# The head of a decoder layer: weight splits placed between evictions of normalised rows, a tile of x fetched sooner, normalisation moved to ScalarE

## The chip, the core and the metric

The kernel runs on one core of one Trainium2 chip. The time is that of one execution on the device, in microseconds, as the median of several runs. A core has a matrix engine (TensorE, PE in the profile), VectorE (DVE), ScalarE (ACT), GpSimd (POOL), a queue for transfers (SyncE, SP) and 16 DMA engines. Each engine works through its own list of instructions in order; semaphores connect the lists.

## The reference

One layer of a hybrid decoder in float32, 512 tokens of width 1024. The input is normalised, and the normalised rows `h` go through one wide input projection, whose columns are split among gated linear attention, latent attention and gates; an MLP and two more normalisations follow.

```python
def layer_norm(x, g, b):
    mu = jnp.mean(xf, axis=-1, keepdims=True)
    var = jnp.mean(jnp.square(xf - mu), axis=-1, keepdims=True)
    return ((xf - mu) * lax.rsqrt(var + LN_EPS) * g + b).astype(x.dtype)
...
h = layer_norm(x, ln_in_g, ln_in_b)
...
q_g, k_g, v_g, r_g, a_lr, q_lat, kv_lat, gate_logits = jnp.split(h @ w_in, offsets, axis=-1)
```

The change touches only what happens up to the first of these projections: the normalisation of the input, its transposition, and the preparation of the first weights.

## The kernel before

**Tiles.** The 512 tokens are four tiles of 128 rows and 1024 columns, `xt[0]` to `xt[3]`. TensorE needs the normalised rows transposed, so that the 1024 channels stand in eight blocks `k` of 128 partitions. `hT[k]` holds block `k` for all 512 tokens, as two matrices: `h` is kept as a high part, rounded to the matrix engine's float format (fp32r), and a low part, the rest. Weights are kept the same way. Each product is three matmuls: high by high, high by low and low by high (in the first projection lines 284, 285 and 286).

**Normalising a tile** (`ln_rows`, L428). VectorE takes the statistics of both halves of the row (L431), joins them (L432) and adds epsilon (L433); GpSimd takes the power -1/2 (L434). Then the row is scaled: on VectorE in one instruction (L440), or, with `on_act`, on ScalarE (L438) after VectorE has made the bias (L437). Before the change tile 0 goes to ScalarE and the others to VectorE.

**Transposing** (`ln_transpose`, L442). For two tiles at a time (256 tokens) and for each block `k`, two transposes (L449) fill a PSUM bank, named `px`, or `mm` for `k` = 4 and 5 of the first two tiles. Four `px` banks and four `mm` banks exist. Then the bank is evicted: ScalarE writes the high part of `hT[k]` with gain and bias (L452, tile `h`), a second copy `lnt` in full precision comes from VectorE (L456) or, in the first two tiles at odd `k`, from ScalarE (L454), and VectorE subtracts the two for the low part (L457).

**Weights.** `stream` is the list of all weight pieces in the order of use. `fetch(n)` asks for the transfers of the first `n` on the SP queue (L176, tile `wraw`, three buffers); `pump(i)` makes the splits as far as allowed ahead of piece `i`: ScalarE rounds the high part (L191), VectorE subtracts for the low part (L192). The first projection (`lat`, 720 columns in two parts of 360, in four pieces of two blocks each) keeps its eight split pieces in `xh` and `xl`; later pieces go to `whi` and `wlo`. A `wraw` buffer is free for the next transfer when both splitting instructions have read it. `st["gates"]` lists instructions behind which the next split has to stand on its engine; `tc.issue_after` does this.

**The order.** The code is traced once. A planner that comes with the language gives every engine its list from this order and from its own estimates of time, so an instruction that is written later can stand earlier on its engine if nothing binds it. Generators such as `ln_in1` are advanced one step between groups of matmuls (`tick`). The code of the head is, in this order: `pump(-1)` (L470: two pieces fetched and split), `ln_in0` (L471: tiles 0 and 1 normalised, transposed and evicted), three copies of the unit matrix (L474 to L477), then the first projection for tiles 0 and 1, under which `ln_in1` (L1098) loads tiles 2 and 3, normalises and transposes them, and then the same projection for tiles 2 and 3. `prep` (L496) makes masks and the tables of the rotary embedding; its first instructions are bound behind `last_in`, the low part of block 3 of tiles 0 and 1.

Of the kernel before, what the change touches and what calls it, by code (L numbers as in the profile page):

```python
# [19 lines left out]
P = 128  # L20
# [32 lines left out]
def tile_hybrid_block(ctx: ExitStack, tc: tile.TileContext, I, out, dbg=None):  # L53
# [39 lines left out]
    def f(ap):  # L93
        return ap.bitcast(F32)
# [39 lines left out]
    identr = consts.tile([P, P], F32R, name="identr")  # L134
# [5 lines left out]
    st = {"dma": 0, "spl": 0, "gates": ()}  # L140
# [38 lines left out]
    def pump(i):  # L179
        fetch(i + 1 + DMA_AHEAD)  # L180
        while st["spl"] < min(len(stream), i + 2 + SPLIT_AHEAD):
            e = stream[st["spl"]]
            if st["spl"] > i + e.get("ahead", SPLIT_AHEAD) and not e["res"]:
                break
            nk, n = e["nk"], e["n"]
            hi, lo = [A([P, nk, T * 2 // nk], F32R, w) for w in HOME["a" if e["res"] else e.get("home", "w")]]
            raw = e["src"]() if "src" in e else e.pop("raw")
            with ExitStack() as gates:
                for g in st["gates"]:
                    gates.enter_context(tc.issue_after(g.ins))  # L190
                st["ins"] = act(hi[:, :nk, :n], raw[:, :nk, :n], AF.Copy)  # L191
                st["lo"] = vtt(lo[:, :nk, :n], raw[:, :nk, :n], f(hi[:, :nk, :n]), op=ALU.subtract)  # L192
            st["gates"] = ()
            e["w"] = (hi, lo)
            if "post" in e:
                e["post"](raw)
            if "post2" in e:
                later[st["spl"] + 2] = lambda p=e["post2"], r=raw: p(r)
            later.pop(st["spl"], lambda: None)()
            st["spl"] += 1  # L200
# [227 lines left out]
    def ln_rows(src, dst, mv, on_act=False):  # L428
# [4 lines left out]
        vts(mv[:, 1:2], mv[:, 1:2], LN_EPS, None, op0=ALU.add)  # L433
        gtt(mv[:, 1:2], mv[:, 1:2], mhalf[:, 0:1], op=ALU.pow)  # L434
        if on_act:
            nmr = S([P, 1], F32, "nmr")
            stt(nmr, mv[:, 0:1], -1.0, mv[:, 1:2], op0=ALU.mult, op1=ALU.mult)  # L437
            act(dst, src, AF.Identity, scale=mv[:, 1:2], bias=nmr)  # L438
        else:
            vts(dst, src, mv[:, 0:1], mv[:, 1:2], op0=ALU.subtract, op1=ALU.mult)  # L440

    def ln_transpose(rows, g, b, outs, hf, alt=False, n="h0"):  # L442
        tk = slice(hf * 256, (hf + 1) * 256)
        for k in range(NK):
# [7 lines left out]
            ha = act(hi, p[:, :256], AF.Identity, scale=g[:, k:k + 1], bias=b[:, k:k + 1])  # L452
            if (alt or n == "h1") and k % 2:
                act(tmp, p[:, :256], AF.Identity, scale=g[:, k:k + 1], bias=b[:, k:k + 1])  # L454
            else:
                vts(tmp, p[:, :256], g[:, k:k + 1], b[:, k:k + 1], op0=ALU.mult, op1=ALU.add)  # L456
            hd = vtt(lo, tmp, f(hi), op=ALU.subtract)  # L457
            if n == "h1":
                st["ln"] = (ha, hd)
            yield hd  # L460
# [4 lines left out]
    def ln_in0():  # L465
        for tt in range(2):
            ln_rows(xt[tt], xt[tt], mvin[:, tt, :], on_act=tt == 0)
        yield from ln_transpose(xt, g_in, b_in, hT, 0, alt=True)

    pump(-1)  # L470
    last_in = list(ln_in0())[3]  # L471


    act(identr, ident, AF.Copy)  # L474
# [21 lines left out]
    def prep():  # L496
        with tc.issue_after(last_in.ins):
# [600 lines left out]
    def ln_in1():  # L1098
        for i in range(4):
            if i == 0:  # L1100
                load_x(2)
            if i == 2:
                load_x(3)
            yield
        with tc.issue_after(last_in.ins):
            for tt in (2, 3):
                ln_rows(xt[tt], xt[tt], mvin[:, tt, :])
        yield
        yield from ln_transpose(xt, g_in, b_in, hT, 1, alt=False)
# [604 lines left out]
```

## Time and profile before

| | us |
|---|---|
| median of 3 runs | 872.87 |
| lowest and highest of them | 872.13, 873.47 |
| the profiled execution, its own time | 873.01 |
| span of the profiled execution, first to last instruction | 871.2 |
| PE busy | 854.2 |
| VectorE busy | 635.0 |
| ScalarE busy | 470.6 |

The profile is of one execution. Its span is 1.8 us shorter than the time of the same execution. Times in its views count from the start of the span. In a timeline row stand the start, the time that the merged instructions took, the engine, the line and operation, and out<-in by the names of the tiles; in square brackets the idle time of the engine before it and what ended it. In a group's row stand, behind the bar, the busy time, the mean of one in ns, and the idle time ahead of the group. In a row of the waits stand the total, the number and the longest.

### The profile page before, as it was taken

To read this page: it belongs to the slowest core of one execution; us is meant where nothing else is said; L and a number is where in the kernel's file an instruction comes from. 1 tells how busy PE (TensorE), PEld (TensorE's weight loads), DVE (VectorE), ACT (ScalarE), POOL (GpSimd) and SP (SyncE) were. 2 spreads that over 40 slices of the span, in tenths; PEclk is the share of its full clock that TensorE was granted. 3 is DMA by queue.
4 is the path that set the end of the run, shared out by engine and by line. 5 is a ranking of instruction groups with operands and counts; after the bars stand their busy time and mean duration, and the time that the engine had idled before them with its cause. 6 is when DMAs were issued, how large, how long until landed. Compare 5 with 4: busy or idle time off the path is not lost.

```text
span 871.2 us, 12821 instructions
## 1 busy us (share of the span) xinstructions
PE 854.2 (98%) x4757; PEld 746.3 (86%) x4757; DVE 635.0 (73%) x1045; ACT 470.6 (54%) x829; POOL 146.0 (17%) x184
## 2 busy tenths in 40 slices
PE   5999999999999999999999999999999999999996
PEld 5988888889999988888888888988888888889985
DVE  7859989978567547567766887986567646888865
ACT  6546777656475625355545333575366446666820
POOL 0323304221110030300000022005300520141000
PEclk9999999999999999999999999999999999999999
DMA  7994946695656434322126445008922990499311
GB/s 243 280 238 146 324 161 169 169 320 189 145 156 155 148 93 121 79 62 97 49 96 252 140 144 216 1 0 240 264 77 49 284 223 24 98 242 229 114 67 73
DMA packets 95214, 134.58 MB, mean 154 GB/s; under 512 B 12672, under 2 KB 58112, under 8 KB 95152
## 3 DMA queue, kind: packets, MB, share of 16 engines
q1 hardware_dynamic: 73840, 92.36, 33.2%
q0 software_dynamic: 19392, 37.76, 20.4%
q10 hardware_dynamic: 1920, 3.66, 1.1%
q8 instruction: 37, 0.61, 0.3%
q14 instruction: 25, 0.20, 0.1%
HBM read 110.15 MB, written 8.91 MB: 137 GB/s over the span
## 4 chain that ended last, share of the span: by engine, by line
PE 97%; DVE 1%; ACT 1%; DMA 1%; POOLq 0%; issue 0%; SPq 0%; DVEq 0%
PE mm L248 11%; PE mm L249 11%; PE mm L250 11%; PE mm L286 5%; PE mm L285 5%; PE mm L284 5%; PE mm L1240 4%; PE mm L1239 4%; PE mm L1238 4%; PE px L1527 2%; PE px L1525 2%; PE px L1526 2%; PE mm L1527 2%; PE mm L1525 2%; PE mm L1526 2%; PE mm L755 1%
## 5 line engine op out<-in xcount | busy, mean ns | idle before, releaser
L192 DVE TENSOR_TENSOR wlo<-wraw,whi 128x1024 fp32r<-128x1024 f32 (+1 forms) x90 | 98.7, 1098 | 83.2 <-ACT whi L191 75.0
L191 ACT ACTIVATE whi<-wraw 128x1024 fp32r<-128x1024 f32 (+1 forms) x90 | 85.5, 950 | 80.9 <-PE mm L249 42.7
L249 PE MATMUL mm<-h,whi 128*128 128x512 f32 x224 | 87.2, 389 | 0.0
L248 PE MATMUL mm<-h,whi 128*128 128x512 f32 x224 | 86.9, 390 | 0.0
L250 PE MATMUL mm<-h,wlo 128*128 128x512 f32 x224 | 83.4, 390 | 0.0
L192 DVE TENSOR_TENSOR wlo<-wq,whi 128x1024 fp32r<-128x1024 f32 x44 | 53.8, 1223 | 28.4 <-ACT whi L191 28.1
L1544 POOL DMA_DIRECT2D res<-ev x42 | 37.4, 1018 | 181.8 <-ACT ev L1542 148.3
L191 ACT ACTIVATE whi<-wq 128x1024 fp32r<-128x1024 f32 x44 | 46.5, 1058 | 27.4 <-PE mm L1239 17.1
L1240 PE MATMUL mm<-sh,wlo 128*128 128x256 f32 x176 | 50.0, 284 | 0.0
L1238 PE MATMUL mm<-sh,whi 128*128 128x256 f32 x176 | 50.0, 284 | 0.0
L1239 PE MATMUL mm<-sh,whi 128*128 128x256 f32 x176 | 49.8, 283 | 0.0
L250 PEld LDWEIGHTS mm<-h,wlo 128*128 128x128 f32 x224 | 42.0, 188 | 9.1 <-DVE wlo L192 0.4
L249 PEld LDWEIGHTS mm<-h,whi 128*128 128x128 f32 x224 | 42.1, 188 | 8.8
L248 PEld LDWEIGHTS mm<-h,whi 128*128 128x128 f32 x224 | 42.1, 188 | 8.6
L191 ACT ACTIVATE xh<-wraw 128x1024 fp32r<-128x1024 f32 (+1 forms) x28 | 27.1, 981 | 28.5 <-PE mm L286 16.5
L192 DVE TENSOR_TENSOR xl<-wraw,xh 128x1024 fp32r<-128x1024 f32 (+1 forms) x28 | 31.2, 1128 | 7.7 <-ACT xh L191 7.7
L1587 ACT ACTIVATE relu<-mm 128x512 f32<-128x512 f32 x24 | 14.2, 594 | 41.2 <-PE mm L250 41.2
L1240 PEld LDWEIGHTS mm<-sh,wlo 128*128 128x128 f32 x176 | 33.8, 192 | 0.0
L1239 PEld LDWEIGHTS mm<-sh,whi 128*128 128x128 f32 x176 | 33.8, 192 | 0.0
L1238 PEld LDWEIGHTS mm<-sh,whi 128*128 128x128 f32 x176 | 33.8, 192 | 0.0
L1238 PE MATMUL mm<-h,whi 128*128 128x256 f32 x112 | 32.0, 286 | 0.0
L1240 PE MATMUL mm<-h,wlo 128*128 128x256 f32 x112 | 31.9, 284 | 0.0
(495 smaller groups left out, 2701.2 us busy)
## 6 DMA issues: line engine op xcount, KB each, us to landing
wraw<-in_w_ff_dram SPq DMA_DIRECT2D x36, 512.0 KB, 4.8
wraw<-in_w_in_dram SPq DMA_DIRECT2D x30, 512.0 KB, 4.7
wq<-in_w_ff_dram POOLq DMA_DIRECT2D x26, 512.0 KB, 9.8
res<-ev POOLq DMA_DIRECT2D x42, 256.0 KB, 9.2
wq<-in_w_in_dram SPq DMA_DIRECT2D x20, 512.0 KB, 7.3
wq<-in_w_in_dram POOLq DMA_DIRECT2D x18, 512.0 KB, 9.8
hsd<-hs SPq DMA_DIRECT2D x16, 256.0 KB, 4.1
xr<-hsd SPq DMA_DIRECT2D x16, 256.0 KB, 5.1
```

The source lines that it names most:

```text
L191: st["ins"] = act(hi[:, :nk, :n], raw[:, :nk, :n], AF.Copy)
L192: st["lo"] = vtt(lo[:, :nk, :n], raw[:, :nk, :n], f(hi[:, :nk, :n]), op=ALU.subtract)
L248: mm(o, hi[:, c], xh, start=k == 0, stop=False)
L249: mm(o, hi[:, c], xl, start=False, stop=False)
L250: mm(o, lo[:, c], xh, start=False, stop=k == nk - 1)
L284: mm(o, xh, hi[:, :n], start=opens, stop=False, skip_group_check=share)
L285: mm(o, xh, lo[:, :n], start=False, stop=False, skip_group_check=share)
L286: mm(o, xl, hi[:, :n], start=False, stop=last, skip_group_check=share)
L1238: mm(oa, hi[:, k, c], xh, start=opens and k == 0 and a == 0, stop=False, skip_group_check=True)
L1239: mm(oa, hi[:, k, c], xl, start=False, stop=False, skip_group_check=True)
L1240: mm(oa, lo[:, k, c], xh, start=False, stop=k == 3, skip_group_check=True)
L1544: nc.gpsimd.dma_start(res[tt + t][:, j * T:(j + 1) * T], e, accum_op=ALU.add)
```

## The change

- `split_next` is cut out of `pump`: it makes one split. Ahead of the first normalisation there is one split instead of two, while three pieces are fetched instead of two.
- Tile 2 of x is asked for right behind these three (`load_x(2)`), ahead of the fourth weight piece, and tile 3 at the first step of `ln_in1`.
- `st["turns"]` is a list of gates, one for each coming split: split 1 stands behind the eviction of block 1 of tiles 0 and 1 (on both engines), split 2 behind that of block 3, split 3 behind that of block 5, split 4 is free. Later ones are bound behind the statistics of tiles 2 and 3 and behind blocks 3 and 5 of these tiles' evictions.
- In the first two tiles the evictions are bound to their written order on each engine (`run` in `ln_transpose`).
- `ln_rows` has `to`: columns below it are scaled on VectorE, the others on ScalarE. Tile 0 goes to ScalarE whole, tile 1 is cut in half, tiles 2 and 3 go to ScalarE whole.
- `lnt` of odd blocks comes from ScalarE for tiles 2 and 3 too.
- The statistics of tiles 2 and 3 are bound behind the low half of the split that was traced last; `prep` is bound behind the low part of the last block of tiles 2 and 3.
- `identr`, a copy of the unit matrix that nothing reads, is gone.

```diff
-    st = {"dma": 0, "spl": 0, "gates": ()}
+    st = {"dma": 0, "spl": 0, "gates": (), "turns": []}
...
+            split_next()
+
+    def split_next():
+        e = stream[st["spl"]]
+        nk, n = e["nk"], e["n"]
+        if st["turns"]:
+            st["gates"] = st["turns"].pop(0)
...
-    def ln_rows(src, dst, mv, on_act=False):
+    def ln_rows(src, dst, mv, to=D):
...
-        vts(mv[:, 1:2], mv[:, 1:2], LN_EPS, None, op0=ALU.add)
+        var = vts(mv[:, 1:2], mv[:, 1:2], LN_EPS, None, op0=ALU.add)
         gtt(mv[:, 1:2], mv[:, 1:2], mhalf[:, 0:1], op=ALU.pow)
-        if on_act:
+        if to < D:
             nmr = S([P, 1], F32, "nmr")
             stt(nmr, mv[:, 0:1], -1.0, mv[:, 1:2], op0=ALU.mult, op1=ALU.mult)
-            act(dst, src, AF.Identity, scale=mv[:, 1:2], bias=nmr)
-        else:
-            vts(dst, src, mv[:, 0:1], mv[:, 1:2], op0=ALU.subtract, op1=ALU.mult)
+            act(dst[:, to:], src[:, to:], AF.Identity, scale=mv[:, 1:2], bias=nmr)
+        if to:
+            vts(dst[:, :to], src[:, :to], mv[:, 0:1], mv[:, 1:2], op0=ALU.subtract, op1=ALU.mult)
+        return var
 
     def ln_transpose(rows, g, b, outs, hf, alt=False, n="h0"):
         tk = slice(hf * 256, (hf + 1) * 256)
+        done = {}
+
+        def run(fn, *a, **kw):
+            with ExitStack() as gates:
+                if alt and fn in done:
+                    gates.enter_context(tc.issue_after(done[fn].ins))
+                i = fn(*a, **kw)
+            done.update({act: i} if fn is act else {vts: i, vtt: i})
+            return i
...
-            ha = act(hi, p[:, :256], AF.Identity, scale=g[:, k:k + 1], bias=b[:, k:k + 1])
-            if (alt or n == "h1") and k % 2:
-                act(tmp, p[:, :256], AF.Identity, scale=g[:, k:k + 1], bias=b[:, k:k + 1])
+            ha = run(act, hi, p[:, :256], AF.Identity, scale=g[:, k:k + 1], bias=b[:, k:k + 1])
+            if k % 2:
+                ha = run(act, tmp, p[:, :256], AF.Identity, scale=g[:, k:k + 1], bias=b[:, k:k + 1])
             else:
-                vts(tmp, p[:, :256], g[:, k:k + 1], b[:, k:k + 1], op0=ALU.mult, op1=ALU.add)
-            hd = vtt(lo, tmp, f(hi), op=ALU.subtract)
+                run(vts, tmp, p[:, :256], g[:, k:k + 1], b[:, k:k + 1], op0=ALU.mult, op1=ALU.add)
+            hd = run(vtt, lo, tmp, f(hi), op=ALU.subtract)
...
-            ln_rows(xt[tt], xt[tt], mvin[:, tt, :], on_act=tt == 0)
+            ln_rows(xt[tt], xt[tt], mvin[:, tt, :], to=tt * T)
         yield from ln_transpose(xt, g_in, b_in, hT, 0, alt=True)
 
-    pump(-1)
-    last_in = list(ln_in0())[3]
-
-
-    act(identr, ident, AF.Copy)
+    fetch(3)
+    load_x(2)
+    split_next()
+    evs = list(ln_in0())
+    last_in = evs[7][1]
+    st["turns"] = [evs[k] for k in (1, 3, 5)] + [()]
...
     def prep():
+        last_in = evs[-1][1]
...
     def ln_in1():
-        for i in range(4):
-            if i == 0:
-                load_x(2)
-            if i == 2:
-                load_x(3)
-            yield
-        with tc.issue_after(last_in.ins):
-            for tt in (2, 3):
-                ln_rows(xt[tt], xt[tt], mvin[:, tt, :])
-        yield
-        yield from ln_transpose(xt, g_in, b_in, hT, 1, alt=False)
+        load_x(3)
+        yield
+        for tt, wait in ((2, 3), (3, 2)):
+            for _ in range(wait):
+                yield
+            with tc.issue_after(st["lo"].ins):
+                st["turns"].append((ln_rows(xt[tt], xt[tt], mvin[:, tt, :], to=0),))
+        st["turns"].append(())
+        yield
+        for k, e in enumerate(ln_transpose(xt, g_in, b_in, hT, 1, alt=False)):
+            evs.append(e)
+            if k in (3, 5):
+                st["turns"].append(e)
+            yield
```

34 lines of the change are left out of this document (16 added, 18 removed).

## The prediction

> **What bounds the kernel now.** I read the page first. Its first part says that TensorE is busy in nearly all of the span:
>
> ```profile
> PE 854.2 (98%) x4757; PEld 746.3 (86%) x4757; DVE 635.0 (73%) x1045; ACT 470.6 (54%) x829; POOL 146.0 (17%) x184
> ```
>
> 871.2 us of span less 854.2 leaves 17 us. A busy PE need not be at its peak, so the view of the waits comes next, for PE alone and over the whole span:
>
> ```profile
> PE px L449 <- ACT x L438: 8.8, 1, 8.8
> PE px L1046 <- DVE PT L112: 0.4, 1, 0.4
> PE mm L248 <- ACT h L452: 0.3, 1, 0.3
> PE mm L248 <- DVE rt L1000: 0.2, 1, 0.2
> PE px L449 <- DVE lnt L456: 0.2, 1, 0.2
> ```
>
> PE waits 8.8 us for the first normalised tile, 0.2 us more in the head (for the evictions `lnt`), and 0.9 us in all the rest of the program. Whatever the change moves, it can win only where PE isn't already fed, and that is before about 15 us. So the head is read in order of time, PE's timeline first (start, time with the modelled end, engine, line, what):
>
> ```profile
> 8.81 1.11 PE L449 MATMUL px<-ca,x 128*128 128x128 f32 x4 [8.81 <-ACT x L438]
> 9.71 0.63 PE L449 MATMUL mm<-ca,x 128*128 128x128 f32 x2
> 10.22 1.11 PE L449 MATMUL px<-ca,x 128*128 128x128 f32 x4
> ...
> 11.41 0.65 PE L284 MATMUL mm<-xh,h 128*128 128x360 f32 x1
> 11.86 0.50 PE L285 MATMUL mm<-xl,h 128*128 128x360 f32 x1
> 12.16 0.50 PE L284 MATMUL mm<-xh,h 128*128 128x360 f32 x1
> 12.46 0.50 PE L285 MATMUL mm<-xl,h 128*128 128x360 f32 x1
> 13.13 1.14 PE L449 MATMUL px<-ca,x 128*128 128x128 f32 x4 [0.17 <-DVE lnt L456]
> 13.92 0.82 PE L286 MATMUL mm<-xh,h 128*128 128x360 f32 x2
> 14.57 0.33 PE L284 MATMUL mm<-xh,h 128*128 128x360 f32 x1
> 14.74 0.33 PE L285 MATMUL mm<-xl,h 128*128 128x360 f32 x1
> ```
>
> Two things are to be seen. First, the pace: from start to start a 360-column matmul takes 0.30 us at 11.86 and 12.16, and 0.17 us at 14.57. Up to about 14.3 us PE goes at half pace, whatever it is given. Second, the gaps at that pace: 11.41 to 11.86 is 0.45 (0.15 too long), 12.46 to 13.13 is 0.67 (0.37 too long), and from 13.13 to 14.57, where four transposes and two matmuls stand, some 0.15 are lost. Before 10.22 about 0.1 is lost: two transposes at 0.23 each, (9.71 - 8.81) / 4, from 9.71 would be over at 10.16, and the matrix waits for tile 1. In all 0.75 us of waiting, at half pace.
>
> What they wait for stands in the timelines of ScalarE and VectorE:
>
> ```profile
> 7.51 1.24 ACT L438 ACTIVATE x<-x,nmr,mvin 128x1024 f32<-128x1024 f32 x1 [2.14 <-DVE nmr L437]
> 8.66 2.17 ACT L191 ACTIVATE xh<-wraw 128x720 fp32r<-128x720 f32 x3
> 10.74 1.92 ACT L452 ACTIVATE h<-px,ca 128x256 fp32r<-128x256 f32 x4
> ...
> 13.44 1.05 ACT L454 ACTIVATE lnt<-px,ca 128x256 f32<-128x256 f32 x2
> ```
>
> ```profile
> 9.18 0.98 DVE L440 TENSOR_SCALAR x<-x,mvin 128x1024 f32<-128x1024 f32 x1 [0.67 <-POOL mvin L434]
> 10.09 2.53 DVE L192 TENSOR_TENSOR xl<-wraw,xh 128x720 fp32r<-128x720 f32 x3
> 12.54 0.99 DVE L456 TENSOR_SCALAR lnt<-px,ca 128x256 f32<-128x256 f32 x2
> 13.45 0.75 DVE L457 TENSOR_TENSOR h<-lnt,h 128x256 fp32r<-128x256 f32 x2
> ...
> 15.75 1.28 DVE L431 BATCH_NORM_STATS2 bst<-x 128x6 f32<-128x512 f32 x2
> ```
>
> Three weight splits run on each engine ahead of the evictions. On VectorE they hold the first `lnt` until 12.54, and with it the PSUM banks that the last four transposes (13.13) and the low halves that the L286 matmuls (13.92) need.
>
> After 14.5 us PE is fed without a gap. The groups of PE from 14.5 to 46 us, and one piece of the critical chain that gives the transposes' full pace:
>
> ```profile
> L285 PE MATMUL mm<-xl,h 128*128 128x360 f32 x60 | 19.8, 332 | 0.0
> L284 PE MATMUL mm<-xh,h 128*128 128x360 f32 x60 | 18.9, 326 | 0.0
> L286 PE MATMUL mm<-xh,h 128*128 128x360 f32 x62 | 18.7, 336 | 0.0
> L449 PE MATMUL px<-ca,x 128*128 128x128 f32 x16 | 2.6, 271 | 0.0
> ```
>
> ```profile
> 25.92 0.44 PE px L449 x4
> ```
>
> 182 matmuls at 0.165 and 16 transposes at 0.11 are 31.8 us: the whole of the 31.5 us window (those at its ends are counted). Nothing done to tiles 2 and 3 can win time here. It can only lose some.
>
> **The change part by part.** *Tile 1 on two engines.* The 1024 columns took VectorE 0.98 us. For 512 the cost isn't in the trace; from below it is the 0.41 of a 256-column row (the two L457 took 0.75 with overlap), from above 0.98; I take 0.6. One small instruction for the bias goes ahead of it, about 0.1. VectorE's half is ready near 9.9 instead of 10.16, but PE is with tile 0's six transposes until about 10.1, so the gain is 0.1 us at half pace. ScalarE's half, between 0.5 (an eviction of 256 columns, 1.92 / 4) and 1.24 us, goes behind the one split that still stands there (2.17 / 3 = 0.72, so from 8.66 to 9.4) and ends near 10.2. It is wanted by the fifth bank only, and delays no eviction that could have started: the first bank is full near 10.5.
>
> *Splits 1 to 3 behind evictions 1, 3 and 5.* Of the three splits ahead of the evictions on VectorE (2.53 us, 0.84 each) one stays. The first `lnt` then starts near 10.7 to 10.8, not at 12.54, and the transposes of the last two blocks can go near 11.4. ScalarE's first `h` could go at 10.6, where it now goes at 10.74. So PE's first projection matmul stays near 11.3 (tile 1's six transposes from 10.1 at 0.21 to 0.23 each keep PE until then), but the 0.15, the 0.37 and the 0.15 behind it close. At half pace block 0 (six matmuls, 1.8 us) and the last four transposes (0.9) are enough work to carry PE from 11.4 to 14.1; block 1 needs only the split already made.
>
> *What that is worth.* 0.75 us filled at half pace are 0.75 x 0.165 / 0.30 = 0.41 us of work at full pace that doesn't have to be done later. From below it is worth nothing (if PE's order lets the gaps stand elsewhere), from above 0.75. I take 0.35, as the filled time isn't all of one kind.
>
> *Is the supply quick enough behind it?* PE wants a pair of blocks every 12 x 0.165 = 1.98 us from 14.6 on. ScalarE per pair: three evictions of 0.48 and a split of 0.72 is 2.16 us. VectorE per pair: one `lnt` of 0.50, two differences of 0.37 and a split of 0.84 is 2.1 us. Both are slower than PE, yet both start near 10.6, four us ahead. ScalarE: 10.6 + 12 x 0.48 + 3 x 0.72 = 18.5; VectorE: 10.8 + 4 x 0.50 + 8 x 0.37 + 3 x 0.84 = 18.3. PE, eight matmuls in at 14.6, is at the last block's low half near 14.6 + 36 x 0.165 = 20.5. A margin of 2 us hides the gates: cost nothing. Without that cover each microsecond late is a microsecond of PE.
>
> *Transfers.* The SP queue, and a window of the transfers:
>
> ```profile
> 2.11 9.26 SPq L176 DMA_DIRECT2D wraw<-in_w_in_dram  x4
> 11.41 0.47 SPq L126 DMA_DIRECT2D x<-in_x_dram  x1
> ```
>
> ```profile
> 9.50:12.00 2.50, 2.50 (x12) 2.23 (x12) 2.50 (x4) 2.50 (x5) 0.12 (x1) 1.00 0.01 2
> ```
>
> The fourth weight transfer waits in the queue until the first split frees its buffer, and tile 2 is queued behind it (11.41). Asked for ahead of that one, tile 2 moves while the DMA engines do nothing (share 0.01 from 9.5 to 12). It stands behind three weight transfers, of which only the first is wanted before 10 us. On the other side the next weight buffers come free later, as splits 1 to 3 are later by 1 to 5 us. PE wants the fifth split at 14.6 + 40 x 0.165 = 21.2, and its transfer is asked for when split 1 is over, near 13.4. I count nothing.
>
> *Tiles 2 and 3 on ScalarE.* VectorE loses two normalisations and, with odd blocks of the second half evicted on ScalarE, four `lnt`; ScalarE gains 2 x 1.24 + 4 x 0.5 = 4.5 us. From 18 to 38 us ScalarE has room for it; its idle time ahead of its groups there:
>
> ```profile
> L452 ACT ACTIVATE h<-px,ca 128x256 fp32r<-128x256 f32 x8 | 4.1, 566 | 2.5 <-PE px L449 2.5
> L191 ACT ACTIVATE xh<-wraw 128x720 fp32r<-128x720 f32 x3 | 2.4, 804 | 3.2 <-DMA wraw<-in_w_in_dram 3.2
> L191 ACT ACTIVATE whi<-wraw 128x1024 fp32r<-128x1024 f32 x2 | 2.1, 1070 | 2.4 <-DMA wraw<-in_w_in_dram 2.4
> L550 ACT ACTIVATE lat<-mm 128x360 f32<-128x360 f32 x2 | 0.9, 474 | 1.2 <-PE mm L286 1.2
> ```
>
> 2.5 + 3.2 + 2.4 + 1.2 = 9.3 us. The small casts of `prep` (one of them below) now stand behind the last eviction of the second half; VectorE has gained more there than they cost, and PE's next users of them come many microseconds later.
>
> ```profile
> 21.64 0.39 DVE L500 CAST lmask<-lmi 128x448 uint8<-128x448 int32 x1
> ```
>
> The copy for `identr` ran before the first tile was in; removing it gives nothing.
>
> *The sum.* 873.01 (the profiled execution) - 0.35 = 872.66. The median of the runs shown is 0.14 under the profiled execution, so 872.5.
>
> **The half pace.** The rows say that it ends between 13.92 and 14.57, some 5.4 us after PE's first instruction and 2.9 after its first projection matmul. [...]
>
> **The rivals.** *No gain (872.9).* The gates only say what a split may not come before. If PE's order, written out beforehand, keeps the same waits in other places, or the filled half pace is used for work that wasn't late, the 0.35 is gone. For it: PE started its projection at 11.41 and will again start near there. Against it: the 0.37 at 12.46 has a plain cause that is removed.
>
> *VectorE falls behind (slower, 874.9).* VectorE now takes its evictions strictly in order, each waiting for ScalarE's, and the statistics of tile 2, which lands sooner, may come in between. Two tiles' statistics are 2 x 1.28 and some 0.8 of small ones: 18.3 + 3.4 = 21.7, against 20.5 where PE wants the last low half: 1.2 us; the next split, 0.84, is wanted at 21.2 and is over at 22.6: 1.4 in all. With 0.3 us per pair for the turns between the two engines, 0.9 more: 2.3 lost, 0.35 won, 872.9 + 2.0 = 874.9. It decides from the point where VectorE's last difference ends after 20.5. Against it: the statistics wait for a split's low half, and the margin of 2 us covers one tile's.
>
> [...]
>
> **How the numbers follow.** About 0.2% (1.75 us) is what a measurement of this kernel can tell from no change; the three runs shown lie 1.34 us apart. Chances: forecast 0.56, no gain 0.18, VectorE behind 0.15, sooner full pace 0.11. The forecast's and the no-gain case lie within 0.2%. Faster by more: 0.11; slower by more: 0.13, as a small part of that case (a stall under 1.7 us) stays within; the same: 0.76. The forecast's own range, with a gain of 0 to 0.75 and the spread of the runs, is 871.7 to 873.4. To leave out no more than 2 in 10 it reaches to 870.9 on the one side, where the sooner pace lies, and to 874.4 on the other, part of the way to the late VectorE.
>
> **What would show it.** Right: the first `lnt` on VectorE near 10.8, the last four of the first 16 transposes near 11.4 to 12, no gap over 0.1 us between projection matmuls from 11.4 on, eight to nine of them started by 14.6, tile 2's transfer ahead of the fourth weight transfer, and still no PE wait from 15 to 46 us. Wrong: a PE wait on `xl` or `h` between 15 and 22 us, a point of full pace that has moved by over 0.5 us, or a change of more than 1 us that comes from a stage behind 46 us, where only the order of the instructions could have brought it.

## The result, and the profile after

The kernel after takes 878.68 us (median of 4 runs, 878.30 to 879.22), the kernel before beside it 873.17 (4 runs, 872.13 to 874.82): a ratio of 1.0061, with an interval of 1.0046 to 1.0076. The forecast was 872.5, with a range of 870.9 to 874.4 and 0.13 for slower. It was wrong: the change costs 5.5 us.

The profiled execution after took 879.22 us, its span is 877.4, 6.2 more than before. First the page's line of busy times, which says how little of this is work:

```profile
PE 855.0 (97%) x4757; PEld 746.0 (85%) x4757; DVE 632.4 (72%) x1042; ACT 475.2 (54%) x835; POOL 146.0 (17%) x184
```

PE is busy 0.8 us longer with the same 4757 instructions; VectorE gave up 2.6 us and ScalarE took 4.6, as the change meant. The other 5.4 us are waits. The view of PE's waits over the whole span (total, number, longest):

```profile
PE px L464 <- DMA wraw<-in_w_in_dram: 10.0, 1, 10.0
PE mm L255 <- DVE wlo L197: 1.5, 1, 1.5
PE mm L1260 <- ACT u L1276: 0.9, 1, 0.9
PE mm L290 <- DVE xl L197: 0.8, 2, 0.6
PE px L889 <- ACT M L833: 0.6, 1, 0.6
...
PE mm L289 <- ACT h L456: 0.3, 1, 0.3
PE px L873 <- DVE sd L112: 0.3, 1, 0.3
...
```

The rows left out (`PT`, `rt` and `h` for L253) are as before. Set beside the five rows of before, there are three lots. The first wait grew from 8.8 to 10.0: 1.2. In the head, `xl` (0.8) and one `h` (0.3) are new and `lnt` (0.2) is gone: 0.9. And four waits are new far behind the head, where the change edits nothing: `wlo` 1.5, `u` 0.9, `M` 0.6 and `sd` 0.3, together 3.3, at 73, 241, 147 and 191 us. 1.2 + 0.9 + 3.3 is the 5.4.

PE executes the same number of matmuls in both, so the start of its n-th matmul can be set beside that of before too. After is behind by 1.2 us at the first matmul, by 0.5 near 17 us, by 2.3 at 50 to 66 us and by 6.2 at the end. So the head costs 1.05 us beyond the late first start, and the stages behind 66 us cost 4.0: each late wait delays PE a little more than it lasts (behind the 1.55 us at 73 us it is 1.59 further behind, behind the 0.94 at 242 us 1.1).

**The first wait** is no work of the change. Its row names a weight transfer, but what PE's first transposes (L464) read is tile 0 as ScalarE has scaled it, and that was over at 9.96:

```profile
8.72 1.24 ACT L443 ACTIVATE x<-x,nmr,mvin 128x1024 f32<-128x1024 f32 x1 [3.87 <-DVE nmr L442]
```

VectorE's timeline in the head:

```profile
7.93 0.69 DVE L436 BATCH_NORM_STATS2 bst<-x 128x6 f32<-128x512 f32 x1 [1.78 <-DMA x<-in_x_dram]
8.54 0.14 DVE L442 SCALAR_TENSOR_TENSOR nmr<-mvin 128x1 f32<-128x1 f32 x1
...
10.47 0.64 DVE L445 TENSOR_SCALAR x<-x,mvin 128x512 f32<-128x512 f32 x1
...
12.40 0.54 DVE L456 TENSOR_SCALAR lnt<-px,ca 128x256 f32<-128x256 f32 x1 [0.48 <-ACT h L456]
```

Before, in the same view:

```profile
6.73 0.69 DVE L431 BATCH_NORM_STATS2 bst<-x 128x6 f32<-128x512 f32 x1 [0.26 <-DMA x<-in_x_dram]
```

Tile 1 of x landed 1.2 us later than in the profile of before, and VectorE's list keeps the bias `nmr` of tile 0 (8.54) behind tile 1's first statistics (7.93), and with it ScalarE's scaling and PE's first transpose. Among all profiles of this case tile 1 landed between 6.2 and 7.9 us, with tile 2 asked for early or late, and in the others PE's first wait was 8.3 to 9.0. Part of the 6.2 us is thus this one execution; the medians differ by 5.5.

**The head** does what the prediction said up to about 15 us. PE's timeline after, over the stretch shown of before:

```profile
10.01 1.11 PE L464 MATMUL px<-ca,x 128*128 128x128 f32 x4 [10.01 <-DMA wraw<-in_w_in_dram]
...
13.53 0.50 PE L290 MATMUL mm<-xl,h 128*128 128x360 f32 x1
13.83 1.05 PE L464 MATMUL px<-ca,x 128*128 128x128 f32 x4
...
15.08 0.34 PE L289 MATMUL mm<-xh,h 128*128 128x360 f32 x1
...
24.82 0.43 PE L290 MATMUL mm<-xl,h 128*128 128x360 f32 x1 [0.22 <-DVE xl L197]
27.65 0.43 PE L290 MATMUL mm<-xl,h 128*128 128x360 f32 x1 [0.60 <-DVE xl L197]
```

The step of 0.67 us ahead of the last transposes (12.46 to 13.13 before) is 0.30 now (13.53 to 13.83), and from PE's first start to the matmul of 15.08 it is 5.07 us, where 14.57 of before stood 5.76 behind its own first start: 0.7 won. About half of that is the full pace, which began sooner. In the rows it begins between 4.8 and 5.1 us after PE's first start, before between 5.4 and 5.8. With 0.30 us a matmul at half pace and 0.165 at full pace, 0.8 us sooner are worth 0.8 x (1 - 0.165 / 0.30) = 0.37 us, by estimate.

Then the head loses: `xl` at 24.8 and 27.65, where PE had waited for nothing.

**Those two** come from late weight pieces and from the change's own gates. The SP queue after:

```profile
4.75 0.47 SPq L126 DMA_DIRECT2D x<-in_x_dram  x1
11.95 4.28 SPq L175 DMA_DIRECT2D wraw<-in_w_in_dram  x2
...
17.93 10.07 SPq L175 DMA_DIRECT2D wraw<-in_w_in_dram  x5
```

And of before, behind the rows already shown:

```profile
11.99 1.02 SPq L176 DMA_DIRECT2D wraw<-in_w_in_dram  x2
```

Tile 2 goes ahead of the fourth piece, as intended. But the fifth piece is now asked for by 16.2 (11.95 + 4.28), and before the fifth and sixth were both asked for by 13.0. ScalarE, in the same execution after, stands waiting for its pieces:

```profile
14.07 0.82 ACT L196 ACTIVATE xh<-wraw 128x720 fp32r<-128x720 f32 x1
...
20.55 0.81 ACT L196 ACTIVATE xh<-wraw 128x720 fp32r<-128x720 f32 x1 [1.08 <-DMA wraw<-in_w_in_dram]
22.62 0.81 ACT L196 ACTIVATE xh<-wraw 128x720 fp32r<-128x720 f32 x1 [1.26 <-DMA wraw<-in_w_in_dram]
23.84 0.81 ACT L196 ACTIVATE xh<-wraw 128x720 fp32r<-128x720 f32 x1 [0.41 <-DMA wraw<-in_w_in_dram]
```

PE waits for the low halves, though, and these stand behind the statistics on VectorE, as the change's gates demand:

```profile
22.22 1.28 DVE L436 BATCH_NORM_STATS2 bst<-x 128x6 f32<-128x512 f32 x2
...
23.85 0.91 DVE L197 TENSOR_TENSOR xl<-wraw,xh 128x720 fp32r<-128x720 f32 x1
24.68 1.28 DVE L436 BATCH_NORM_STATS2 bst<-x 128x6 f32<-128x512 f32 x2
...
26.69 0.91 DVE L197 TENSOR_TENSOR xl<-wraw,xh 128x720 fp32r<-128x720 f32 x1
```

The `xl` of 23.85 had its high half at 23.43 (22.62 + 0.81) and began when tile 2's statistics were over: both causes share the wait of 0.22. The `xl` of 26.69 had its high half at 24.65, two microseconds earlier, and began when tile 3's were over: the wait of 0.60 is the gate's, and a sooner transfer wouldn't have shortened it.

**The late waits** are the larger lot. The one at 73 us on PE:

```profile
74.83 0.50 PE L255 MATMUL mm<-h,wlo 128*128 128x512 f32 x1 [1.55 <-DVE wlo L197]
75.16 0.40 PE L253 MATMUL mm<-h,whi 128*128 128x512 f32 x1
75.40 0.39 PE L254 MATMUL mm<-h,whi 128*128 128x512 f32 x1
```

VectorE and GpSimd there, after:

```profile
69.06 3.50 DVE L1143 TENSOR_TENSOR hraw<-h 128x512 f32<-128x512 f32 x2
72.47 2.30 DVE L197 TENSOR_TENSOR wlo<-wraw,whi 128x1024 fp32r<-128x1024 f32 x1
```

```profile
69.00 1.30 POOL L647 TENSOR_TENSOR g<-g,az 128x512 f32<-128x512 f32 x1 [10.24 <-ACT az L644]
70.46 5.47 POOL L647 TENSOR_TENSOR g<-g,az 128x512 f32<-128x512 f32 x3 [0.16 <-ACT az L644]
```

and before:

```profile
66.29 2.38 DVE L1121 TENSOR_TENSOR hraw<-h 128x512 f32<-128x512 f32 x2
68.60 2.32 DVE L192 TENSOR_TENSOR wlo<-wraw,whi 128x1024 fp32r<-128x1024 f32 x1
```

```profile
66.74 6.76 POOL L628 TENSOR_TENSOR g<-g,az 128x512 f32<-128x512 f32 x4 [7.38 <-ACT az L625]
```

```profile
70.97 0.50 PE L250 MATMUL mm<-h,wlo 128*128 128x512 f32 x1
```

GpSimd makes four subtractions for the gates (`GL`, in `latents`) in both. VectorE's sums `hraw` and the split `wlo` take longer beside them: after, two sums took 1.28 us at 66.27 with GpSimd idle and 3.50 at 69.06, and the split 2.30, where it takes 1.22 with the subtractions off GpSimd (in a run below). Before, `wlo` was over at 70.92 and PE used it at 70.97: it came just in time. After, both of the two sums lie under GpSimd's work instead of the greater part of them (3.50 us instead of 2.38), the split is over at 74.77, and PE waits. So the stretch had 0.05 us of slack, and something shifted GpSimd's four against VectorE's list. What shifted them is the matter of the experiments.

### The profile page after: what moved, and what is told of

Read it like the earlier page. It is cut to its first block, busy times and chain, and to the rows that moved or that the text cites. A ratio compares the mean times of both kernels' runs of the same rounds, so it can differ in the third digit from the quotient of the medians.

```text
span 877.4 us, 12831 instructions
## 1 busy us (share of the span) xinstructions
PE 855.0 (97%) x4757; PEld 746.0 (85%) x4757; DVE 632.4 (72%) x1042; ACT 475.2 (54%) x835; POOL 146.0 (17%) x184
## 4 chain that ended last, share of the span: by engine, by line
PE 89%; DVE 3%; DMA 3%; issue 2%; ACT 1%; POOL 1%; POOLq 0%; DVEq 0%; ACTq 0%
PE mm L253 11%; PE mm L254 11%; PE mm L255 11%; PE mm L290 5%; PE mm L289 5%; PE mm L291 5%; PE mm L1260 4%; PE mm L1261 4%; PE mm L1262 4%; PE px L1547 2%; PE px L1549 2%; PE px L1548 2%; DMA wraw<-in_w_in_dram 2%; PE mm L1547 2%; PE mm L1549 2%
## 5 line engine op out<-in xcount | busy, mean ns | idle before, releaser
L253 PE MATMUL mm<-h,whi 128*128 128x512 f32 x224 | 86.9, 390 | 0.0
L255 PE MATMUL mm<-h,wlo 128*128 128x512 f32 x224 | 83.6, 391 | 1.5 <-DVE wlo L197 1.5
L255 PEld LDWEIGHTS mm<-h,wlo 128*128 128x128 f32 x224 | 42.0, 188 | 10.7 <-DVE wlo L197 2.0
L253 PEld LDWEIGHTS mm<-h,whi 128*128 128x128 f32 x224 | 42.1, 188 | 8.6
```

The costliest lines, as they stand in the source:

```text
L253: mm(o, hi[:, c], xh, start=k == 0, stop=False)
L255: mm(o, lo[:, c], xh, start=False, stop=k == nk - 1)
```

## The experiments

Three theories stood at first: the early tile 2 delays tile 1 (X), the gates of the placed splits hold up transfers (G), and the late `prep` lets the planner write another order (O). Later theory O had to be parted from mere lateness of `prep` (L). In all runs the median is set beside that of the kernel before on the same chip. "Late waits" are the four above.

**The kernel before once more**, for the scatter.

> The kernel before, once more, for a second profile. Theory S (the landing of the second tile of x varies by itself between executions): it lands more than 0.5 us away from the 6.7 us of the first profile, and PE's first instruction (8.81) moves with it. Theory X (in the changed kernel the early transfer of tile 2 delays it): it lands within 0.3 us of 6.7 here, PE starts near 8.8. Time 872 to 874 us by both.

873.89 us with a span of 872.1; PE's first transpose at 8.64, tile 1 of x landed at 6.54. None of the four late waits, but PE waits 0.5 us for `SD` at 192 us, which the first profile of this kernel doesn't have. That wait, which some kernels below have too, is thus scatter of the execution and no work of a change.

**Tile 2 asked for late again, all else as after.**

```diff
     fetch(3)
-    load_x(2)
     split_next()
...
     def ln_in1():
+        load_x(2)
         load_x(3)
```

> The changed kernel with tile 2 of x asked for at the first step under the projection, where the kernel before has it; all else stays. Theory X: tile 1 lands near 6.7 us and PE starts near 8.8 instead of 10.0, so about 1.2 us come back: 877.4. Theory G (the splits behind the evictions free the weight buffers late, and the later weight pieces land late): PE still waits about 2 us on xl and h between 20 and 35 us. Theory S: PE's start has nothing to do with this edit. Theory P (most of the loss behind 46 us comes from the order that the planner writes out, which any edit of the head changes): the waits at 73, 147 and 241 us (1.5, 0.6 and 0.9 us) change in size without a cause in the edit.

880.71 against 873.16 (1.0067 to 1.0107). Tile 2 landed at 20.65, the head's waits became more (`xl` 1.1 in three, `xh` 0.7), the late waits stayed. The early tile 2 doesn't cost here; without it the change is no faster.

**Two splits ahead of the evictions, no gates for the next ones.**

```diff
     split_next()
+    split_next()
     evs = list(ln_in0())
     last_in = evs[7][1]
-    st["turns"] = [evs[k] for k in (1, 3, 5)] + [()]
+    st["turns"] = []
```

> The changed kernel with two splits ahead of the evictions and without the gates on splits 1 to 4, as in the kernel before; tile 2 of x early, normalisation on ScalarE and the strict order of the evictions stay. Theory G: the weight transfers 4 and 5 are asked for near 12 us again, the waits between 20 and 35 us go, about 2 us come back: 876.5. Theory X: PE still starts near 10.0. Theory P: the waits behind 46 us change in size, without a cause in the edit.

877.71 against 873.16 (1.0042 to 1.0072). Tile 1 landed at 6.80 and PE began at 8.90, with tile 2 still asked for early, so theory X falls. The head's waits were 0.6 (`xh`) and 0.3 (`h`), and the late ones were all there: the gates of splits 1 to 4 (G) explain part of the head at most, and nothing behind it.

**Before, with tile 2 asked for early alone.**

```diff
+    fetch(3)
+    load_x(2)
     pump(-1)
...
             if i == 0:
-                load_x(2)
-            if i == 2:
                 load_x(3)
```

> The kernel before with one edit: three weight pieces and tile 2 of x are asked for ahead of the first splits. Theory X: tile 1 lands 1 us later, PE starts near 10.0, time 874.3 or more. Theory S or none: PE starts within 0.3 us of 8.8 and the time is within 0.7 us of before, 872.2 to 873.9. Theory P: even this small edit changes waits behind 46 us by more than 0.5 us.

877.42 against 873.16 (1.0030 to 1.0063): alone, this part costs 4.3 us, and by another way than expected. ScalarE's and PE's timelines:

```profile
27.09 1.06 ACT L191 ACTIVATE whi<-wraw 128x1024 fp32r<-128x1024 f32 x1 [8.15 <-DMA wraw<-in_w_in_dram]
28.05 0.79 ACT L191 ACTIVATE xh<-wraw 128x720 fp32r<-128x720 f32 x1
```

```profile
28.89 1.27 PE L284 MATMUL mm<-xh,h 128*128 128x360 f32 x3 [2.34 <-ACT xh L191]
```

The planner put a split for a later stage (`whi`) ahead of the `xh` split that PE needs next; its piece of weights came late, and ScalarE stood 8.15 us behind it. Then a second loss follows. In a table of windows (window, length, busy time of PE, its weight loads, VectorE, ScalarE and GpSimd, granted clock, share of DMA, GB/s):

```profile
28.60:32.00 3.40, 3.11 (x10) 2.82 (x11) 3.40 (x7) 3.11 (x7) 0.00 (x0) 0.50 0.44 106
```

The clock is 0.50 for 3.4 us right behind the wait. PE is busy for 3.1 of these, and at half pace (0.30 us a matmul instead of 0.165) that costs about 1.5 us, by estimate. 2.3 of wait, 1.5 of half clock and another 0.5 of `h` are 4.3, which is what was measured. There are no late waits here.

**Before, with the placed splits and the strict order of evictions alone.**

```diff
-    pump(-1)
-    last_in = list(ln_in0())[3]
+    fetch(3)
+    split_next()
+    evs = list(ln_in0())
+    last_in = evs[3][1]
+    st["turns"] = [evs[k] for k in (1, 3, 5)] + [()]
```

(with `split_next` and `run` as in the change).

> The kernel before with the placed splits alone: one split ahead, splits 1 to 3 behind evictions 1, 3 and 5, evictions of the first two tiles in strict order. Theory G: weight pieces 4 to 6 land 3 to 5 us later than before, PE waits about 2 us between 20 and 35 us, time 875. If the late waits came from this part, PE waits again at 73, 146, 190 and 241 us and the time is 878; by theories N and Q they are absent.

875.56 against 873.14 (1.0015 to 1.0034). No late waits. VectorE and PE, and a window behind:

```profile
20.19 1.28 DVE L437 BATCH_NORM_STATS2 bst<-x 128x6 f32<-128x512 f32 x2 [0.88 <-DMA x<-in_x_dram]
...
21.80 0.85 DVE L198 TENSOR_TENSOR xl<-wraw,xh 128x720 fp32r<-128x720 f32 x1
```

```profile
22.71 0.51 PE L291 MATMUL mm<-xl,h 128*128 128x360 f32 x1 [1.77 <-DVE mvin L439]
```

```profile
22.90:26.30 3.40, 3.40 (x12) 3.40 (x12) 3.40 (x7) 1.60 (x3) 0.45 (x1) 0.50 0.57 130
```

The statistics of tile 2 stand ahead of the split `xl` on VectorE, and tile 2, queued behind the weight piece that now waits for its gate, landed at 20.17. PE waits 1.8 us, and the half clock follows again. 11 matmuls in that stretch at half pace are again about 1.5 us by estimate, so wait and half clock cost 3.3, more than the 2.4 measured; the filled gaps ahead of them had won some 1.0 in this profile, relative to PE's first start. In the order that the planner made here, the placed splits lose without tile 2 early, and tile 2 early loses without the gates (the run before this): each part alone costs time.

**Before, with the moves to ScalarE alone.**

```diff
-            ln_rows(xt[tt], xt[tt], mvin[:, tt, :], on_act=tt == 0)
+            ln_rows(xt[tt], xt[tt], mvin[:, tt, :], to=tt * T)
...
-                ln_rows(xt[tt], xt[tt], mvin[:, tt, :])
+                ln_rows(xt[tt], xt[tt], mvin[:, tt, :], to=0)
...
-            if (alt or n == "h1") and k % 2:
+            if k % 2:
```

> The kernel before with the moves to ScalarE alone: tile 1 cut between the engines, tiles 2 and 3 normalised on ScalarE, the second copies of odd blocks of tiles 2 and 3 on ScalarE. Theory O: as the bound of the preparation stays, the first latents' matmul stays at position 265 or before, no late waits, 873 to 874.5; the head may lose up to 1 us where ScalarE's splits and these moves meet. Theory N2 (the moves are harmful by themselves): late waits as in the changed kernel, 876 or more.

876.33 against 873.02 (1.0026 to 1.0056). Head waits on `h` of 0.9 (VectorE's) and 0.7 (ScalarE's), 0.5 on `SD` near 190 us (the scatter of the first run), none of the four late ones. Its 3.3 us are more than these 2.1; where the rest lies is not shown.

**After, with the normalisation of tiles 1 to 3 and the odd `lnt` back on VectorE.**

```diff
-            ln_rows(xt[tt], xt[tt], mvin[:, tt, :], to=tt * T)
+            ln_rows(xt[tt], xt[tt], mvin[:, tt, :], to=tt * D)
...
-            if k % 2:
+            if (alt or n == "h1") and k % 2:
...
-                st["turns"].append((ln_rows(xt[tt], xt[tt], mvin[:, tt, :], to=0),))
+                st["turns"].append((ln_rows(xt[tt], xt[tt], mvin[:, tt, :]),))
```

> The changed kernel with the normalisation of tiles 1, 2 and 3 whole on VectorE and the second copy of odd blocks of tiles 2 and 3 on VectorE, as in the kernel before; the placed splits, the early tile 2 and the bound of the small preparation stay. Theory N (the moves to ScalarE make the late waits at 73, 146, 190 and 241 us, which the changed kernel and its two variants so far share to 0.03 us, by putting GpSimd's and VectorE's later work over each other in another way): these waits go, and 3 to 4 us come back: 875. Theory Q (they come from the bound of the small preparation behind the last eviction): they stay as they are, 1.5, 0.6, 0.3 to 1.1 and 0.9 us, and the time stays within 1 us of 878.7. Theory G: the waits between 20 and 35 us stay (2 us) by both.

873.69 against 873.14 (0.9997 to 1.0016). The four late waits are gone, with `prep` still bound late; the waits on `xl` (0.8) stay, and the one on `SD` (0.5) is there.

**After, with `prep` bound early as before.**

```diff
     def prep():
-        last_in = evs[-1][1]
+        last_in = evs[3][1]
```

> The changed kernel with the small preparation (masks, the tables of the rotary embedding) bound behind block 3 of tiles 0 and 1, as in the kernel before. Theory Q: the latents' chain starts earlier against the projections, VectorE's sums at 66 to 74 us fall on GpSimd's four long additions as they did before, the waits at 73, 146 and 241 us go, 3 to 4 us come back: 875. Theory N: they stay, 878.7 within 1 us.

873.77 against 873.14 (0.9996 to 1.0015): one line takes the cost from 5.5 us to 0.6, which can't be told from no change. PE's waits behind 46 us:

```profile
PE px L889 <- DVE SD L838: 0.5, 1, 0.5
PE px L1065 <- DVE PT L112: 0.4, 1, 0.4
PE mm L253 <- ACT h L456: 0.3, 1, 0.3
PE mm L253 <- DVE rt L1019: 0.2, 1, 0.2
```

None of the four is left (the `SD` is that of the first run); the waits in the head (`xl` 0.8, `h` 0.3) are. The lists hold the same instructions after and in this variant, but on PE some 200 of about 4700 stand at another place, on VectorE some 80 and on ScalarE some 40. The piece that matters for what follows ("+" is after, "-" this variant; L629 are the matmuls of the gates, whose results GpSimd's four subtractions work on, L253 to L255 those of the second projection):

```
 L255 MATMUL mm_605<-h_19_134,wlo_433 128x512
+L253 MATMUL mm_602<-h_22_142,whi_432 128x512
+L254 MATMUL mm_602<-h_22_142,whi_432 128x512
 L629 MATMUL px_661<-aT_201,wa_202 128x512
 L629 MATMUL px_667<-aT_201,wa_202 128x512
-L253 MATMUL mm_602<-h_22_142,whi_432 128x512
-L254 MATMUL mm_602<-h_22_142,whi_432 128x512
```

After, the gates' matmuls stand two places later, 268 instead of 266.

**Before, with `prep` bound late alone.**

```diff
     def prep():
+        last_in = evs[-1]
```

> The kernel before with the small preparation bound behind the last eviction of tiles 2 and 3, and nothing else. Theory Q: the head is as before (no PE wait between 15 and 46 us), the late waits of 1.5, 0.6, 0.3 to 1.1 and 0.9 us at 73, 146, 190 and 241 us appear, 876 to 877. Theory N: no late waits, 873.2 within 0.7 us.

873.90 against 873.14 (0.9998 to 1.0017). The gates' matmuls stay at 266, no late waits. The late bound alone doesn't bring the late waits, and its cost can't be told from none: they need the moves to ScalarE too (with these undone, two runs above, they were gone as well).

**After, with `prep` bound behind block 3 of the second half** instead of its last.

```diff
     def prep():
-        last_in = evs[-1][1]
+        last_in = evs[11][1]
```

> The changed kernel with the small preparation bound behind block 3 of tiles 2 and 3, between the two bounds tried (behind block 3 of tiles 0 and 1: 873.8, behind the last block: 878.7). Theory L (lateness: the later the preparation, the more is lost): a time between, 875 to 877, with late waits of a size between. Theory O (order: the planner puts the latents' matmuls two places later on PE, position 267 for the first instead of 265, and the rest follows from that): the time is either near 873.8 or near 878.7, and goes with that position.

873.66 against 873.02 (0.9996 to 1.0015). 266 again, no late waits. PE's list has 2 instructions at another place than that with the early bound, VectorE's 6. `prep`'s first cast to `lmask` runs at 33.3 here, at 40.9 after and at 19.0 with the early bound: it is late, which speaks for the order (O) and against lateness (L). The next run but one decides it.

**After, with the four subtractions on VectorE instead of GpSimd.**

```diff
-            gtt(GL[h], GL[h], azs[h], op=ALU.subtract)
+            vtt(GL[h], GL[h], azs[h], op=ALU.subtract)
```

> The changed kernel with the four additions of the latents' chain that stand on GpSimd near 69 to 76 us put on VectorE, all else equal. Theory C (the 1.5 us wait at 73 us is made there: VectorE's sums and the weight split behind them, 0.68 and 1.22 us alone, take 1.78 and 2.30 beside these additions, and in the changed kernel one more of them stands ahead of the split): the wait at 73 us goes, the sums take 0.7 us each, 1.5 us come back: 877.2; the waits at 146, 190 and 241 us, which have additions of their own on GpSimd, stay if they are separate, and shrink too if they are a follow-up of the first. Rival: the wait stays at 1.5 us, as VectorE is late for another reason.

876.79 against 873.02 (1.0029 to 1.0059). VectorE at that place:

```profile
68.09 1.28 DVE L1143 TENSOR_TENSOR hraw<-h 128x512 f32<-128x512 f32 x2
69.29 1.22 DVE L197 TENSOR_TENSOR wlo<-wraw,whi 128x1024 fp32r<-128x1024 f32 x1
```

With GpSimd out of the way the two sums take 1.28 us instead of 3.50, the split 1.22 instead of 2.30, and the wait at 73 us is gone. That shows the mechanism of this one wait. The other late ones stay: `sd` 1.1, `u` 0.9, `M` 0.5; the gates' matmuls are at 268. They are there in all four kernels with these waits (after, the two runs with tile 2 late and with two splits ahead, and this one), and at 266 in all others. `sd` is 0.3 in the profile of after and 1.1 in the other three.

**After, with only the order turned back.** `prep` stays bound behind the last eviction; the four matmuls that open block 3 of the second projection are bound behind the first two gates' matmuls.

```diff
-            mm(o, hi[:, c], xh, start=k == 0, stop=False)
+            with ExitStack() as gates:
+                if "z" in st:
+                    gates.enter_context(tc.issue_after(st["z"][0].ins)); st["z"][1] -= 1; st["z"][1] or st.pop("z")
+                mm(o, hi[:, c], xh, start=k == 0, stop=False)
...
-            mm(z, wa[:, h * P:(h + 1) * P], aT, start=True, stop=True)
+            zi = mm(z, wa[:, h * P:(h + 1) * P], aT, start=True, stop=True)
+            if h == 1:
+                st["z"] = [zi, 4]
```

> The changed kernel, the preparation bound late as it is, with one edge of order on PE: the four matmuls that open block 3 of the second projection stand behind the first two of the latents' gate matmuls, so that these are two places sooner again. PE's list then differs from that of the variant with the early bound (873.8) in 12 lines of 4652, where the changed kernel's differs in over 700. Theory O (the loss behind 46 us comes with the order that the planner writes from there on): the waits at 73, 146, 190 and 241 us go, 873.8 within 0.7. Theory L (the late preparation itself holds somebody up): they stay, 878 within 1.

874.00 against 873.22 (1.0000 to 1.0019). PE's waits behind 46 us:

```profile
PE px L1070 <- DVE PT L112: 0.4, 1, 0.4
PE mm L256 <- ACT h L459: 0.3, 1, 0.3
PE mm L256 <- DVE rt L1024: 0.2, 1, 0.2
```

All four late waits are gone though `prep` is about as late as in the kernel after (its first cast to `lmask` at 39.7): O holds, L falls. With that one bound nearly the whole list turned back: against the kernel with the early `prep`, PE's has 5 instructions at another place, VectorE's 11, the others none. (The kernel after has some 200 on PE, where the expectation says over 700.) This run also shows what the filled gaps are worth by themselves. Its full pace begins 5.3 to 5.6 us after PE's first start, about as before, and its 24th matmul starts 5.55 us after the first (14.58 less 9.03) against 5.93 before: 0.4 won.

**Four weight buffers**, with `prep` bound early, to see the head without the late transfers. The shared pool had to give one buffer (24 to 23).

```diff
-    TAG_W = {'wraw': 3, 'whi': 2, 'wlo': 2}
+    TAG_W = {'wraw': 4, 'whi': 2, 'wlo': 2}
...
-("A", 24)
+("A", 23)
```

> The changed kernel with the preparation bound as before (873.8 by itself) and a fourth buffer for raw weights, taken from the pool of the general tiles (23 instead of 24). Theory G: weight pieces 3 to 5 no longer wait for the gated splits, the fifth piece lands before 16 us instead of 18.9, the waits on xl at 22 to 26 us (0.8 us by the view of the waits, 1.1 with the pipeline) go; 872.7 if the smaller pool costs nothing. Rival: the waits on xl stay, as it is the split's place on ScalarE or VectorE and not the transfer that is late.

884.24 against 873.02 (1.0114 to 1.0144). The fifth weight piece landed at 13.4 instead of 18.9 and the first wait on `xl` (at 23.2 with three buffers) went. The second stayed with 0.57, at 25.45: its high half was over at 21.8, and VectorE made it at 24.49, behind tile 3's statistics. So an early piece takes away the smaller of the two waits, and the larger is the gate's. Of the head's worth in all the run shows nothing: with the smaller pool PE waits 4.6 us between 770 and 797 us, with a stretch at a granted clock of 0.50 beside it (781.4 to 784.7 us), and there are more waits in other stages.

**Two tries at a better kernel**: the subtractions on VectorE, with `prep` bound early, and in the kernel before.

```diff
-            gtt(GL[h], GL[h], azs[h], op=ALU.subtract)
+            vtt(GL[h], GL[h], azs[h], op=ALU.subtract)
```

> The changed kernel with the early bound of the preparation and the four additions of the latents' chain on VectorE. By theory C the sums and the split beside them take 0.7 and 1.2 us instead of 1.8 and 2.3, but PE waits only 0.2 us there in the kernel before, so at most 0.2 us are won if the order stays; 873.6 within 0.7. If the planner's order turns with this edit too, late waits of other sizes and a time up to 3 us away.

> The kernel before with the four additions on VectorE alone. At most 0.2 us won at 71 us, 872.9 within 0.7, if the planner's order stays; if it turns, late waits and a time up to 3 us longer. It is the control for theory O: an edit that has nothing to do with the head.

874.09 against 873.22 (0.9997 to 1.0017), and 873.38 against 873.22 (0.9996 to 1.0015). Where the split comes in time anyway, taking it out of GpSimd's way wins nothing. No version was faster than the kernel before.

## Why the prediction was wrong

*Tile 1 on two engines* was forecast rightly. VectorE's half took 0.64 us (0.6 was taken), the fifth bank was not held up, and no wait came from it.

*Splits behind evictions* was right in mechanism and in sign. The step of 0.67 us became 0.30, and the head up to about 15 us won 0.7 us against 0.35 forecast (0.75 was the upper bound). About half of the 0.7 goes with the full pace, which began 0.8 us sooner in that execution; no run shows why. In the run with only the order turned back, where it began as before, 0.4 was won. It can be seen only relative to PE's first start, since the absolute times (first `lnt` at 12.40, not 10.8) carry the 1.2 us of tile 1's late landing and the strict order behind it.

*The supply behind it and the transfers* are steps that failed in size: both were put at nothing. "A margin of 2 us hides the gates: cost nothing" leaves out that the fifth and sixth low halves stand behind the statistics of tiles 2 and 3, and PE waited 0.60 us for one of them and 0.22 for the other. "Its transfer asked for when split 1 is over, near 13.4. I count nothing" was by 16.2 in this execution: of the 2.8 us 1.2 are the late start, and the rest is that split 1 stands behind evictions that themselves come later on ScalarE than worked out (it ran at 14.07). ScalarE waited 1.08 and 1.26 us for pieces, and this has a part in the smaller wait alone. With 0.3 for an `h`, these waits and what follows from them took back 1.7 us where 0.7 had been won, so in the profiled execution the head cost 1.05 us net. The five variants of the change without the late waits, the one with four buffers left aside, lie 0.55 to 0.87 us above before in their medians; none of these can be told from no change by itself, but all lie on one side.

*Tiles 2 and 3 on ScalarE* had the room that was counted: with the planner's order as before, the kernel with these moves (873.77) and the one without (873.69) can't be told apart. But the room is a property of the order around it: alone in the kernel before, the moves cost 3.3 us.

*`prep` behind the last eviction* is the step that failed and that decided. "VectorE has gained more there than they cost, and PE's next users of them come many microseconds later" is borne out for the instructions: with `prep` about as late as after, 874.00 is left, which can't be told from before. What it left out is that a bound is also an input to the planner. With the moves to ScalarE, this bound turned the place of the gates' matmuls by two, and with it that of some 200 instructions on PE. By medians against before on the same chip, undoing the turn in three ways took the cost from 5.5 us to 0.6 (bound early), 0.6 (bound in the middle) and 0.8 (order alone): 4.7 to 4.9 us of the 5.5 are the order. In the profile of after the stages behind 66 us hold 4.0 of these, 3.3 in the four waits. In the two other kernels with all four, `sd` waits 1.1 instead of 0.3 and these stages hold 5.8, so the share in a median may well lie between.

The prediction named this as what would make it wrong ("a change of more than 1 us that comes from a stage behind 46 us, where only the order of the instructions could have brought it"), but gave it no rival, no price and no chance. Its slower rival, VectorE falling behind in the head, had the cause of the larger wait at `xl` right (the statistics come in between) and its 2.3 us of loss not far from the 1.7 found, but nothing of what lies behind the head. The lower end of the range, 870.9, and the chance of 0.11 rest on a sooner full pace, a term for which no run shows a cause. What the runs showed: in the profile of after the full pace began 0.8 us sooner, worth 0.37 us by the estimate above, and in the run with only the order turned back 5.3 to 5.6 us after PE's first start, about as before.

**What stays open.** Why the planner turns at exactly this pair of edits was seen only from outside. The wait at 73 us is traced to its instructions; those at 147, 191 and 241 us are shown to come with the order, but not which line of it brings each. For the loss in the head from 15 to 33 us the rows name the gates behind the statistics first and the transfers second, but no run took these gates away alone.

## What to carry to other kernels

Where a planner writes the engines' lists, a bound on a few cheap instructions can move hundreds of others much later, so its price isn't that of the instructions: compare the lists of both kernels before trusting a cost of nothing, and look in the profile for stretches with no slack (a split that is over 0.05 us before PE uses it), since these are where a turned order costs. Undo such a bound first when a change loses time in a stage that it doesn't touch. And parts of one change may hold each other up: here tile 2 early and the placed splits cost 4.3 and 2.4 us alone and, together with the other parts and the order of before, 0.6, which can't be told from nothing.

## What the runs showed of the hardware

**Half the clock behind a short wait.** After 2.3 us without a matmul (before with tile 2 early alone) and after 1.8 us (before with the placed splits alone) PE ran at a granted clock of 0.50 for 3.4 us, with 1.00 in the stretches on both sides. After 1.55 us (at 74.83 in the kernel after) it did not: the granted clock was 1.00 from 74 to 80 us, and from 75.16 on the 512-column matmuls start 0.23 to 0.24 us apart, ahead of the wait 0.23. So in one run a wait of 1.8 us was followed by a loss of another 1.5, by the estimate above. Why the clock fell there and stayed here, no run shows.

**VectorE beside GpSimd.** A sum of two 512-column tiles took VectorE 0.64 us with GpSimd idle (1.28 for two) and 1.75 beside its subtractions (3.50 for two), the split 1.22 and 2.30. That is 1.1 us more for each; what holds VectorE up, no run shows.

**A transfer's landing scatters.** Tile 1 of x, asked for in the first 2.1 us of every execution, landed between 6.2 and 7.9 us (at 6.73 in the profile of before, at 7.93 in that of after), and VectorE's order turned that into 1.2 us of PE's first start in the profile of after.
